# Two broadcast rows of an mLSTM stage, loaded by chunk of 128 tokens in place of by tile of 256

## The chip, the cores and the metric

The kernel runs on one core of a Trainium2 chip. The metric is the device time of one execution in microseconds (us), as the median of several runs. The profile is of one execution. Its engines are called PE (matrix multiplications, with PEld for its weight loads), DVE (VectorE), ACT (ScalarE), POOL (GpSimd) and SP (SyncE, which here issues nearly all DMAs).

## What is computed

The reference applies two blocks to x [1, 2048, 1024], in float32. The first is a gated linear attention block with its own normalization. The second is a hybrid layer: one projection feeds three mixers, an mLSTM, a sliding-window attention and a stick-breaking attention, and their outputs are joined, projected, normed and added to x. The change lies in the mLSTM. For each head it does, chunk by chunk (the kernel takes 128 tokens, the reference 64; the result is the same in exact arithmetic):

```python
b = cumsum(log_f);  dmat = b[t] - b[s] + log_i[s]  (s <= t);  inter = b + m
m_t = max(inter, max_s dmat)
s = (q @ k.T) * exp(dmat - m_t)
num = exp(inter - m_t) * (C @ q) + s @ v;  den = exp(inter - m_t) * (n @ q) + sum(s)
h = num / max(|den|, exp(-m_t))
C, n, m = the state carried to the next chunk, scaled by the factor of its last token
```

Two quantities depend on the query token t: `b - m_t`, and the factor `exp(inter - m_t)`. On the chip the token t lies along the free dimension of the tiles that need them, so each has to be present on all partitions, as a broadcast row: bc0 and bc1.

## The kernel before, in words

The work goes in stages over tiles of T = 256 tokens, NT = 8 tiles a stage: GLA twice, an output projection, then sliding-window attention, mLSTM, stick-breaking attention and the last projection. Nearly all matrix products are taken three times with parts of the numbers (`dense3`, lines 276 to 278), and PE is the engine that is busiest.

In a stage `pipeline` (line 177) runs three generators side by side: `mix(t)`, the recurrent part of tile t, beside `gate(t)` and `dense(t + 1)`, the projections of the same and of the next tile. The generators only set the order in which the program names its instructions. Then a planner, which simulates the time of each instruction, puts them in order on each engine: an instruction that it takes to be ready can go ahead of one that stands earlier in the program and isn't. On the chip each engine, and SP with its DMAs, works through its fixed order and waits where an operand is not there yet.

For the mLSTM, `dense(t)` is `mlstm_dense` (line 1197). It makes u and v, the convolution, and then calls `mlstm_stats` (line 1124), which works on a [4, 2, 128] tile (heads by two chunks). It writes `b - m_t` to the DRAM tensor `rows[0]` (line 1149, 4 KB), adds the carried m and takes the exponential in the same tile, and writes that to `rows[1]` (line 1155, 4 KB). DVE's addition at line 1153 has to wait until the first write has read the tile. Back in `mlstm_dense`, lines 1254 to 1257 load both rows from DRAM with a broadcast over 128 partitions:

```python
bc.append(wk.tile([128, 4, T], F32, name=f"bc{j}", tag=f"bc{j}", bufs=2 - j))
nc.sync.dma_start(bc[j], self.rows[j:j + 1, :, t * T:t * T + T].to_broadcast([128, 4, T]))
```

Each load is 512 KB, in 128 x 4 pieces of 1 KB (256 tokens of one head); `rows` is [2, 4, 2048], so the rows of the heads lie 8 KB apart. bc0 has two buffers, bc1 one. The store of the mLSTM output (line 1302, `yT<-ym`) is on SP too; the loads of the next tiles' hidden states (line 234, hh and hl) are issued by POOL.

`mix(t)` calls `mlstm_chunk` (line 1309) for chunks i = 0 and 1. ACT makes w as four exponentials of bc0 (line 1319, recorded at the helper's line 134), POOL masks it (line 1320), PE makes the scores st (1324), DVE multiplies (1325). POOL makes qw = qT * bc1 (line 1330), and PE adds w @ v (1332) and qw @ C (1334) in the bank nu. POOL scales the old state by the last column of the chunk in bc1 (line 1349), DVE adds the new part (1351). Chunk 0 of tile 0 has no state yet, so it does not read bc1.

qT and kT are copied out of PSUM by ACT for two heads (line 1269) and by DVE for two (line 1271); the PSUM tag qk has one bank, so PE's next products at line 1267 wait for that copy.

Of the kernel before, what the change touches and what calls it, by code (L numbers as in the profile page):

```python
# [8 lines left out]
F32 = mybir.dt.float32  # L9
# [17 lines left out]
def interleave(a, na, b, nb):  # L27
    """run the generators a (na steps) and b (nb steps) side by side"""
    ia = ib = 0
    while a is not None or b is not None:  # L30
        if b is None or (a is not None and ia * nb <= ib * na):
            if next(a, StopIteration) is StopIteration:
                a = None
            ia += 1
        else:
            if next(b, StopIteration) is StopIteration:
                b = None
            ib += 1


class Bank:
    """accumulation groups side by side in one PSUM bank: its first matmul clears the bank"""
# [13 lines left out]
class ConstPool:  # L56
    """single tiles by name"""
# [8 lines left out]
class K:  # L66
# [45 lines left out]
    def open(self, ctx, name, bufs=2, side=None):  # L112
        """SBUF of a phase"""
        return ctx.enter_context(self.tc.tile_pool(name=name, bufs=bufs, side=side, reuse_waits="tile"))

    def psum(self, ctx, name, **banks):
        """the PSUM banks of a phase by tag; mm: beside the two lasting ones"""
        self.banks = banks
        self.pp = ctx.enter_context(self.tc.tile_pool(name="ps_" + name, bufs=1, space=PSUM, reuse_waits="tile"))

    def behind(self, ins, before):
        """issue order on one engine, no wait"""
        self.tc.add_manual_dep(ins, before.name, mybir.DependencyInfo(mybir.DependencyClass.NoSync,
                                                                      mybir.DependencyReason.DATA), reason="table")

    def table(self, name):
        """the activation tables that the following Exp, Ln or Sigmoid use"""
        self.tab = self.nc.scalar.preload_act_table_set(name).ins
        for i in self.acts:
            self.behind(self.tab, i)  # L130
        self.acts = []
# [18 lines left out]
    def weights(self, src, name, stage=None, pool=None, k0=0, k1=None, more=None):  # L150
        """src: DRAM [128, k, n]; returns the hi and lo parts of rows k0 to k1. stage: gives the staging tiles;
        more: DRAM [128, k, m] of further columns"""
# [24 lines left out]
    def pipeline(self, n, load, dense, nd, gate, ng, mix, nm, first, lead=0, nxt=None, pri=0):  # L177
        """beside mix(t) run gate(t, h of t) and dense(t + 1, h of t + 1); load(t) gives h two tiles ahead.
        nd, ng, nm(t): the steps of dense, gate and mix; lead: gate goes first for so many t;
        first: h of tile 0 and its dense, begun or None. nxt: what follows: its load(0), its weights, its dense  # L180
        and the steps of it that go here; returns h, weights and the dense begun"""
# [36 lines left out]
    def ahead(self, steps, n):  # L218
        """the steps, their instructions picked as if they stood n earlier"""
        done = False  # L220
        while not done:
            with self.tc.high_priority(offset=n) if n else nullcontext():
                done = next(steps, StopIteration) is StopIteration
            if not done:
                yield

    def load_hl(self, src):
        """src: DRAM hi and lo [128, NK, T] each"""
        out = []
        for n, d in zip(("hh", "hl"), src):  # L230
            out.append([])
            for j in range(0, NK, 4):
                x = self.hp.tile([128, 4, T], F32R, name=n, tag=n)
                self.nc.gpsimd.dma_start(x, d[:, j:j + 4, :])
                out[-1] += [x[:, i, :] for i in range(4)]
        return out

    def load_h(self, src, pool, n, bufs, tag="hf"):
        """src: DRAM [128, NK, T] -> hi, lo; by n rows"""
        for k in range(0, NK, n):  # L240
            h = pool.tile([128, n, T], F32, name="hf", tag=tag, bufs=bufs)
            self.nc.sync.dma_start(h, src[:, k:k + n, :])
            yield k, h

    def split_h(self, parts, B=None):
        """parts: (k, float32 [128, n, T]) -> hi, lo of them, plus the columns B if given"""
# [17 lines left out]
    def dense3(self, out, a, ca, b, cb):  # L264
        """out = sum over k of a[:, k, ca].T @ b[:, k, cb], float32 from three passes."""
        for _ in self.dense3_steps(out, a, ca, b, cb):
            pass

    def dense3_steps(self, out, a, ca, b, cb):
        """the same, with a stop in the middle"""  # L270
# [9 lines left out]
    def rstd(self, out, ss, n):  # L280
        """out = (ss / n + EPS) ** -0.5"""
# [4 lines left out]
    def silu_col(self, src, n, name):  # L286
        """silu of a [128, n] tile by exp and ln."""
# [8 lines left out]
    def matvec(self, pool, w, c, col0):  # L296
        """acc[p, j] = sum over k of c[k * 128 + p] * w[k * 128 + p, col0 + j], j < 512"""
# [11 lines left out]
    def mod_cols(self, pool, stage, w, c, name, at):  # L309
        """columns: G = g * (1 + scale), B = shift, each [128, NK] (feature k * 128 + p). at: (k, what to do there)"""  # L310
# [43 lines left out]
    def transposed(self, xs, tag):  # L354
        """xs: two [128, D] token tiles -> (k, two rows of 128 features in a PSUM bank)"""
# [8 lines left out]
    def make_h(self, pool, banks, G, B, tags=(("hn", 2),) * 4):  # L364
        """banks: of transposed tokens (already scaled by rstd) -> float32 times the columns G, plus B if given,
        by two rows of 128 features"""
# [15 lines left out]
    def x_rstd(self, wk, i, keep):  # L382
        """token-major x, or its squares, and the rstd of its rows"""
# [20 lines left out]
    def x_normed(self, wk, t, G):  # L404
        """feature-major x times rstd and the columns G, by two rows of 128 features"""
# [12 lines left out]
    def gla_consts(self, wk):  # L418
# [7 lines left out]
        # the gate's low-rank part, token-major: hi, hi, lo, each with a column for the bias  # L426
# [76 lines left out]
    def late_mod(self, wk, j):  # L503
        """512 columns of: gate of block 1, shift, scale and gate of block 2"""
# [28 lines left out]
    def gla_dense(self, wk, t, hs, W, st):  # L533
# [6 lines left out]
        # token-major v and r; the low-rank gate  # L540
# [6 lines left out]
        if t % NT == 0:  # L547
            # its rows from partition 0 and 64: hi, from 32: lo, to meet the gate's hi, lo and hi
# [78 lines left out]
        # v of the second head  # L627
# [8 lines left out]
    def gla_gate(self, wk, t, hs, W, st):  # L636
        """silu of r"""
# [11 lines left out]
    def gla_mix(self, wk, t, st, ST):  # L649
# [4 lines left out]
        # scores of both heads and both 128-token chunks  # L654
# [75 lines left out]
    def units(self, key):  # L730
        """loads of the four weight units of a phase"""
# [3 lines left out]
    def halves(self, W):  # L735
        """units of half the rows -> all rows"""
        return [[a + b for a, b in zip(W[j], W[j + 1])] for j in range(0, len(W), 2)]
# [65 lines left out]
    def fm(self, out, W, c0, hs):  # L803
        """feature-major block: out [128 columns from c0, T]"""
        self.dense3(out, W, slice(c0, c0 + 128), hs, slice(0, T))

    def stack_k(self, ka, kb, pk, cols):
        """pk [128, T]: two heads on the partition halves; their hi and lo parts, each head stacked on 128"""
# [6 lines left out]
    def stack_q(self, qs, pq):  # L815
        """pq [128, T]: two heads on the partition halves. qs [128, 4, T]: by head, hi on both halves;
        then by head, lo on the half of its k's hi, zero on the other"""
# [8 lines left out]
    def qk(self, out, qs, h, qt, ks):  # L826
        """out = q.T @ k of head h; ks: columns of its stacked k"""
# [81 lines left out]
    def stick_rows(self, wk, n, b, q, i, kst, v, zero, y, st, po, bank):  # L909
        """queries n * 128 .. of heads 2b and 2b + 1 against all keys before them, from the last chunk back"""  # L910
# [55 lines left out]
    def silu_exp(self, out, src, tmp):  # L966
        """out = src * sigmoid(src), tmp of the same shape"""
# [156 lines left out]
    def mlstm_stats(self, wk, t, g, mp):  # L1124
        """g: gate pre-activations [128, chunk, 8] of tile t -> per-token exponents by chunk and head:
        for the columns, for the state, exp(-m)"""
# [70 lines left out]
    def mlstm_dense(self, t, hs, W):  # L1197
# [8 lines left out]
        def values():  # L1206
            """v, token-major with a column of ones, and the gates"""
# [47 lines left out]
        for j in range(2):  # L1255
            bc.append(wk.tile([128, 4, T], F32, name=f"bc{j}", tag=f"bc{j}", bufs=2 - j))
            nc.sync.dma_start(bc[j], self.rows[j:j + 1, :, t * T:t * T + T].to_broadcast([128, 4, T]))
        # q and k of each head
# [50 lines left out]
    def mlstm_chunk(self, wk, c, i, st, Cs, hg):  # L1309
        qT, kT, vs, bc, y, mst = st[:6]  # L1310
# [7 lines left out]
        for h in range(4):  # L1318
            self.act(w[:, h, :], bc[0][:, h, tok], AF.Exp, bias=mst[:, i, 0, h:h + 1])
# [8 lines left out]
        if Co is not None:  # L1328
            qw = wk.tile([96, 4, 128], F32, name="qw", tag="qw", bufs=1)
            nc.gpsimd.tensor_tensor(qw, qT[:, :, tok], bc[1][0:96, :, tok], op=OP.mult)  # L1330
# [5 lines left out]
        if not last:  # L1336
# [11 lines left out]
            else:  # L1348
                nc.gpsimd.tensor_tensor(Cn, Co, bc[1][0:96, :, i * 128 + 127:i * 128 + 128].to_broadcast([96, 4, 97]),
# [4 lines left out]
        # h = num / max(|den|, exp(-m)), normed over the head  # L1354
# [61 lines left out]
    def rstd_newton(self, sm, n):  # L1416
        """sm [128, 4]: column 3 = (column 2 / n + EPS) ** -0.5, from the exponent's estimate on"""
# [18 lines left out]
# (index of the padded weight, 128-row block) per mLSTM head of 96 rows  # L1436
# [3 lines left out]
def prep(inp):  # L1440
    """layout only"""
# [83 lines left out]
```

## Time and profile before

| | |
|---|---|
| median of 3 runs | 2237.99 us (2236.0 to 2239.27) |
| span of the profiled execution, first to last instruction | 2235.3 us |
| PE busy | 2131.8 us, 95% |
| mLSTM stage | about 1240 to 1640 us of the span |

The span is of one execution, profiled apart from the three timed runs; its own time outside of the span is not recorded, and the median of the runs is 2.7 us above the span. A "mean ns" or "busy" of an engine counts the instruction alone. "Idle before, releaser" says how long the engine stood still before an instruction and what ended that. A wait is put down to the last thing waited for.

### The profile page before, as it was taken

How to read it: one execution, taken by the hardware profiler on the slowest of the kernel's cores; microseconds unless marked ns; L12 is line 12 of the kernel's file. 1: busy time of each engine (PE TensorE's matmuls, PEld its weight loads, DVE VectorE, ACT ScalarE, POOL GpSimd, SP SyncE). 2: the span in 40 equal slices, each digit the busy share in tenths (PEclk: the TensorE clock that was granted, in tenths of full speed). 3: DMA queues.
4: the chain of work that ended last, by engine and by line, in shares of the span. 5: the costliest groups of instructions: out<-in, count | busy, mean ns of one | idle time of the engine just before them, and what ended most of it. 6: DMA issues, size and time to landing. Idle time of an engine off the chain costs nothing. (4 is left out here: it accounts for less than half of the span.)

```text
span 2235.3 us, 39197 instructions
## 1 busy us (share of the span) xinstructions
PE 2131.8 (95%) x14912; PEld 1902.3 (85%) x14912; DVE 1356.7 (61%) x2517; ACT 902.1 (40%) x2290; POOL 857.7 (38%) x1362
## 2 busy tenths in 40 slices
PE   6999999999999999899999999889799999999998
PEld 6899998899998788797888898888798888777787
DVE  6755756566656466564545455445456688788843
ACT  3534334333333333354545343433445555554411
POOL 3522335322223455553324322232445454573410
PEclk9999999999999999999999999989899999999999
DMA  9522313423322566751214322332441111122252
GB/s 321 178 67 73 126 55 114 123 82 99 91 67 91 195 210 225 241 165 53 90 46 145 98 65 72 84 99 67 121 130 43 44 44 43 44 67 81 67 175 99
DMA packets 122412, 240.00 MB, mean 107 GB/s; under 512 B 13248, under 2 KB 39782, under 8 KB 122224
## 3 DMA queue, kind: packets, MB, share of 16 engines
q1 hardware_dynamic: 108400, 187.17, 27.1%
q0 software_dynamic: 13824, 50.34, 7.1%
q8 instruction: 117, 1.92, 0.4%
q14 instruction: 71, 0.58, 0.1%
HBM read 178.66 MB, written 58.79 MB: 106 GB/s over the span
## 5 line engine op out<-in xcount | busy, mean ns | idle before, releaser
L937 DVE TENSOR_TENSOR_SCAN ke<-ke,zero 128x512 f32<-128x512 f32 (+3 forms) x160 | 186.9, 1182 | 25.9 <-POOL ke L932 14.1
L276 PE MATMUL mm<-hh,u1h 128*128 128x256 f32 x640 | 189.1, 296 | 0.0
L278 PE MATMUL mm<-hh,u1l 128*128 128x256 f32 x640 | 187.9, 294 | 0.0
L277 PE MATMUL mm<-hl,u1h 128*128 128x256 f32 x640 | 186.6, 292 | 0.0
L276 PE MATMUL mm<-u0h,hh 128*128 128x272 f32 (+2 forms) x464 | 155.1, 334 | 5.7 <-POOL hh L260 3.6
L278 PE MATMUL mm<-u0h,hl 128*128 128x272 f32 (+2 forms) x464 | 153.9, 332 | 0.6 <-DVE hl L261 0.4
L277 PE MATMUL mm<-u0l,hh 128*128 128x272 f32 (+2 forms) x464 | 153.6, 331 | 0.0
L276 PE MATMUL mm<-hh,u2h 128*128 128x256 f32 x512 | 147.3, 288 | 0.8 <-DVE gs L564 0.5
L277 PE MATMUL mm<-hl,u2h 128*128 128x256 f32 x512 | 146.4, 286 | 0.0
L278 PE MATMUL mm<-hh,u2l 128*128 128x256 f32 x512 | 145.7, 286 | 0.0
L278 PEld LDWEIGHTS mm<-hh,u1l 128*128 128x128 f32 x640 | 126.0, 197 | 1.3 <-issue 0.9
L276 PEld LDWEIGHTS mm<-hh,u1h 128*128 128x128 f32 x640 | 126.0, 197 | 0.7 <-issue 0.2
L277 PEld LDWEIGHTS mm<-hl,u1h 128*128 128x128 f32 x640 | 125.6, 196 | 0.7 <-issue 0.3
L276 PE MATMUL mm<-u3h,hh 128*128 128x256 f32 (+1 forms) x384 | 124.3, 324 | 0.8 <-DVE vl L546 0.8
L278 PE MATMUL mm<-u3h,hl 128*128 128x256 f32 (+1 forms) x384 | 123.3, 321 | 0.0
L277 PE MATMUL mm<-u3l,hh 128*128 128x256 f32 (+1 forms) x384 | 122.7, 319 | 0.0
L49 PE MATMUL po<-aT,sv 128*64 128x128 f32 x1088 | 108.9, 285 | 6.6 <-DVE aT L952 4.9
L134 ACT ACTIVATE be<-z 128x512 f32<-128x512 f32 (+3 forms) x160 | 86.0, 538 | 68.3 <-PE aT L947 68.0
L276 PE MATMUL mm<-hh,u3h 128*128 128x256 f32 x384 | 110.4, 287 | 0.5 <-POOL u3h L147 0.5
L277 PE MATMUL mm<-hl,u3h 128*128 128x256 f32 x384 | 110.3, 287 | 0.0
L278 PE MATMUL mm<-hh,u3l 128*128 128x256 f32 x384 | 109.3, 285 | 0.2 <-DVE mprev L1189 0.2
L134 ACT ACTIVATE ke<-z 128x512 f32<-128x512 f32 (+3 forms) x160 | 86.1, 541 | 54.8 <-PE z L830 33.1
(419 smaller groups left out, 6983.9 us busy)
## 6 DMA issues: line engine op xcount, KB each, us to landing
hh<-h2Th POOLq DMA_DIRECT2D x48, 512.0 KB, 6.0
hl<-h2Tl POOLq DMA_DIRECT2D x48, 512.0 KB, 5.3
mvw<-in_mod_w SPq DMA_DIRECT2D x48, 256.0 KB
stage<-in_ada_w SPq DMA_DIRECT2D x32, 256.0 KB
xt<-in_x SPq DMA_DIRECT2D x16, 512.0 KB
stage<-in_gla_w SPq DMA_DIRECT2D x32, 256.0 KB
oT<-oT SPq DMA_DIRECT2D x32, 256.0 KB
hf<-hT SPq DMA_DIRECT2D x32, 256.0 KB
```

The lines of the kernel that those rows point to most:

```text
L49: i = self.k.nc.tensor.matmul(out, a, b, start=first is None, stop=stop, skip_group_check=True).ins
L134: i = self.nc.scalar.activation(out, src, func, **kw).ins
L276: mm(out, ah[k][:, ca], bh[k][:, cb], start=(k == 0), stop=False)
L277: mm(out, ah[k][:, ca], bl[k][:, cb], start=False, stop=False)
L278: mm(out, al[k][:, ca], bh[k][:, cb], start=False, stop=(k == NK - 1))
L937: nc.vector.tensor_tensor_scan(ke[:, 0:w][:, ::-1], ke[:, 0:w][:, ::-1], zero.to_broadcast([128, w]), ke[:, w:w + 1], op0=OP.mult, op1=OP.add)
```

## The change

The two rows are loaded by chunk: per tile two loads of bc0 with 128 partitions, [128, 4, 128], and two of bc1 with 96 partitions, in pieces of 512 B. In the program they stand in the order bc0 of chunk 0, bc1 of chunk 0, bc0 of chunk 1, bc1 of chunk 1. Each of the two tags has three buffers of half the size, so the SBUF taken is the same (12 KB a partition). `mlstm_chunk` takes the tiles of its chunk. Nothing else is changed but comments.

```diff
         bc = []
-        for j in range(2):
-            bc.append(wk.tile([128, 4, T], F32, name=f"bc{j}", tag=f"bc{j}", bufs=2 - j))
-            nc.sync.dma_start(bc[j], self.rows[j:j + 1, :, t * T:t * T + T].to_broadcast([128, 4, T]))
+        for i in range(2):
+            ts = slice(t * T + i * 128, t * T + i * 128 + 128)
+            bc.append([])
+            for j, n in ((0, 128), (1, 96)):
+                x = wk.tile([128, 4, 128], F32, name=f"bc{j}", tag=f"bc{j}", bufs=3)
+                nc.sync.dma_start(x[0:n], self.rows[j:j + 1, :, ts].to_broadcast([n, 4, 128]))
+                bc[i].append(x)
...
-        qT, kT, vs, bc, y, mst = st[:6]
+        qT, kT, vs, bcs, y, mst = st[:6]
+        bc = bcs[i]
...
-            self.act(w[:, h, :], bc[0][:, h, tok], AF.Exp, bias=mst[:, i, 0, h:h + 1])
+            self.act(w[:, h, :], bc[0][:, h, :], AF.Exp, bias=mst[:, i, 0, h:h + 1])
...
-            nc.gpsimd.tensor_tensor(qw, qT[:, :, tok], bc[1][0:96, :, tok], op=OP.mult)
+            nc.gpsimd.tensor_tensor(qw, qT[:, :, tok], bc[1][0:96], op=OP.mult)
...
-                nc.gpsimd.tensor_tensor(Cn, Co, bc[1][0:96, :, i * 128 + 127:i * 128 + 128].to_broadcast([96, 4, 97]),
+                nc.gpsimd.tensor_tensor(Cn, Co, bc[1][0:96, :, 127:128].to_broadcast([96, 4, 97]),
```

## Rows read from the trace of the kernel before

**Rows 1.** The page: the span, busy time of PE's two queues and of the other engines (share of the span, instructions).

```profile
span 2235.3 us, 39197 instructions
...
PE 2131.8 (95%) x14912; PEld 1902.3 (85%) x14912; DVE 1356.7 (61%) x2517; ACT 902.1 (40%) x2290; POOL 857.7 (38%) x1362
```

**Rows 2.** The view by windows, the mLSTM stage: the stretch and its length, busy time (and number of instructions) of PE, PEld, DVE, ACT and POOL, the mean granted clock of PE as a share of full speed, the busy share of the DMA engines, GB/s.

```profile
1240.00:1640.00 400.00, 354.46 (x2650) 344.01 (x2649) 194.23 (x423) 155.99 (x461) 125.45 (x179) 0.93 0.35 91
```

**Rows 3.** The view of waits, PE alone, 1240 to 1640 us: who waited for whom, us in total, times, longest.

```profile
PE nu L1334 <- POOL qw L1330: 28.2, 6, 6.7
PE nu L1332 <- DVE w L1325: 8.9, 3, 3.7
PE qk L1267 <- ACT qT L1269: 6.1, 2, 3.2
```

**Rows 4.** The view of waits of the other engines in the same stretch, and of SP's queue from 1257 to 1600 us, with the same columns.

```profile
ACT w L134 <- DMA bc<-rows: 52.3, 8, 9.2
...
POOL Cn L1349 <- DMA bc<-rows: 24.3, 5, 5.8
...
POOL qw L1330 <- DMA bc<-rows: 16.8, 3, 5.8
...
SPq L1257 <- DMA rows<-lfR: 65.5, 16, 7.8
```

**Rows 5.** The time line of SP's queue: start, us to issue, line, what is loaded or stored. First tile 2, then tile 4, 5 and 6. Of the two loads at L1257 the first is bc0, the second bc1; of the two stores, L1149 is rows[0], L1155 rows[1].

```profile
1350.60 0.36 SPq L1257 DMA_DIRECT2D bc<-rows  x1
1351.02 0.50 SPq L1302 DMA_DIRECT2D yT<-ym  x1
1351.57 0.42 SPq L1155 DMA_DIRECT2D rows<-lfR  x1
...
1435.45 0.26 SPq L1149 DMA_DIRECT2D rows<-lfR  x1
1436.69 0.36 SPq L1257 DMA_DIRECT2D bc<-rows  x1
1437.66 0.26 SPq L1155 DMA_DIRECT2D rows<-lfR  x1
1444.13 0.36 SPq L1257 DMA_DIRECT2D bc<-rows  x1
...
1485.49 0.36 SPq L1257 DMA_DIRECT2D bc<-rows  x1
...
1492.94 0.36 SPq L1257 DMA_DIRECT2D bc<-rows  x1
...
1533.26 0.36 SPq L1257 DMA_DIRECT2D bc<-rows  x1
...
1540.85 0.36 SPq L1257 DMA_DIRECT2D bc<-rows  x1
```

**Rows 6.** The time lines of ACT, POOL and PE at the first use of the rows: start, us, line, operation, out<-in, shapes, number of instructions merged, idle time before and what ended it. Tile 4, then POOL's first use of bc1 in tiles 5 and 6.

```profile
1444.95 2.45 ACT L134 ACTIVATE w<-bc,mst 128x128 f32<-128x128 f32 x8 [5.07 <-DMA bc<-rows]
...
1453.81 0.83 POOL L1349 TENSOR_TENSOR Cn<-Cn,bc 96x388 f32<-96x388 f32 x1 [5.78 <-DMA bc<-rows]
...
1455.21 1.25 POOL L1330 TENSOR_TENSOR qw<-qT,bc 96x512 f32<-96x512 f32 x1
...
1456.51 0.74 PE L1334 MATMUL nu<-Cn,qw 96*128 96x97 f32 x2 [6.47 <-POOL qw L1330]
...
1459.97 1.27 POOL L1330 TENSOR_TENSOR qw<-qT,bc 96x512 f32<-96x512 f32 x1 [0.41 <-PE nu L1334]
...
1501.78 0.83 POOL L1349 TENSOR_TENSOR Cn<-Cn,bc 96x388 f32<-96x388 f32 x1 [5.41 <-DMA bc<-rows]
...
1549.07 0.83 POOL L1349 TENSOR_TENSOR Cn<-Cn,bc 96x388 f32<-96x388 f32 x1 [4.74 <-DMA bc<-rows]
```

**Rows 7.** The time lines of ACT and PE in tiles 0 and 1, with the same columns.

```profile
1272.61 0.57 ACT L1269 ACTIVATE qT<-qk 96x512 f32<-96x512 f32 x1
...
1273.23 0.36 PE L1267 MATMUL qk<-cuh,wqh 128*96 128x256 f32 x1 [2.92 <-ACT qT L1269]
...
1314.88 0.57 ACT L1269 ACTIVATE qT<-qk 96x512 f32<-96x512 f32 x1
```

**Rows 8.** The view by windows, with the columns of rows 2: the stream of bc0 in tile 4 with no other load beside it; tile 4's wait and the work after it; the load of bif (after its first us); a store of oT to DRAM in pieces of 512 B.

```profile
1438.00:1443.00 5.00, 5.00 (x45) 4.82 (x44) 1.22 (x5) 0.59 (x1) 1.02 (x1) 1.00 0.42 83
1444.00:1460.00 16.00, 9.53 (x71) 9.37 (x70) 2.59 (x5) 4.37 (x12) 5.58 (x10) 0.76 0.63 166
972.00:973.00 1.00, 1.00 (x9) 1.00 (x10) 0.72 (x3) 0.95 (x2) 1.00 (x3) 1.00 0.05 3
134.90:136.10 1.20, 1.20 (x12) 1.20 (x11) 0.54 (x3) 0.38 (x1) 0.00 (x0) 1.00 0.71 219
```

**Rows 9.** Other broadcasts. From the list of DMA issues (KB each): the gate row of block 1 over 128 partitions in pieces of 4 KB, and bif, 8 numbers over 128 partitions in pieces of 32 B. From the time lines of SP and DVE: the issue of the gate and its first use.

```profile
gate<-gate SPq DMA_DIRECT2D x1, 512.0 KB
...
bif<-in_m_bif SPq DMA_DIRECT2D x1, 4.0 KB
...
750.33 0.50 SPq L740 DMA_DIRECT2D gate<-gate  x1
...
756.17 1.90 DVE L768 TENSOR_TENSOR xr<-mm,gate 128x512 f32<-128x512 f32 x3 [11.73 <-DMA gate<-gate]
```

## The prediction

> **What bounds the kernel now.** The first view is the page: TensorE (PE) is busy for 2131.8 of 2235.3 us and no other engine passes 61% [rows 1]. So time is won or lost only where PE waits, or works at a lower clock. The second view is the row of the mLSTM stage among the windows: in the 400 us from 1240 to 1640 PE is busy for 354.46, so 45.5 us are lost there, and the mean granted clock is 0.93 [rows 2]. The third is the table of PE's waits in that stretch: 28.2 us in six waits of the matmuls at L1334 for qw, 8.9 in three for w, 6.1 in two for the ScalarE (ACT) copy of qT [rows 3]. The reader is to see that all three end in the broadcast rows. POOL's multiplications at L1330 and L1349 wait for DMA bc, and ACT's exponentials wait 52.3 us for it [rows 4]; the ACT copy of qT at 1272.61 and 1314.88 only stands in line behind these exponentials, and PE waits for the copy [rows 7].
>
> The fourth view is the time line of tile 4, for why the rows come late [rows 5, 6]. SP issues bc0 at 1436.69, the write of rows[1] at 1437.66, and bc1 only at 1444.13, since bc1 reads what that write stores: 65.5 us of SP's waits at L1257 are for the DMA of rows [rows 4]. ACT starts at 1444.95, POOL at 1453.81, PE goes on at 1456.51 after 6.47 us. The write of 4 KB took 6.47 us, where the same write of rows[0], with nothing ahead of it, took 1.24 (1435.45 to 1436.69). It waited behind bc0: 512 KB at 83 GB/s, as the window 1438 to 1443 has it [rows 8], are 6.3 us of stream, and 0.97 + 6.47 = 7.44 is that stream plus about 1.2. I call the stream of bc0 6.2 us, which leaves exactly 1.24 beside it. From bc0's issue to POOL's first use of bc1 it is 17.12 us in tile 4, 16.29 in tile 5, 15.81 in tile 6, mean 16.4; from bc1's own issue 9.68, 8.84 and 8.22, mean 8.9, which is a stream of 6.2 and 2.7 beside it [rows 5, 6]. ACT's start is 8.26 after bc0's issue, 6.2 + 2.06.
>
> The single buffer of bc1 is not what holds it. Were it so, SP would wait at L1257 for POOL, whose last use of the old bc1 comes before; its waits there are for the DMA [rows 4].
>
> **The change, part by part.** (1) *The third buffer and the split of tiles* remove waits for a free buffer that do not exist: nothing. (2) *Two issues become four.* Each costs SP 0.37 us [rows 5]. Two of them, 0.74 us, fit in the 0.97 between bc0's issue and that of rows[1], where SP has nothing else: nothing, and 0.4 a tile if the write slips. (3) *bc1 for 96 partitions* removes a quarter of its bytes. (4) *Pieces of 512 B in place of 1 KB.* This is the disputed price. Bytes per tile fall from 1024 to 2 x (256 + 192) = 896 KB, pieces rise from 1024 to 2 x (512 + 384) = 1792. Let S be the stream of one chunk of bc0; bc1's is then 0.75 S.
>
> The trace has no 512 B broadcast, so S has bounds. If bytes rule, S is half of 6.2: 3.1. If pieces rule, S is 6.2. The nearest rows: 83 GB/s in pieces of 1 KB are 81 pieces a us, 12.3 ns each; the broadcast bif, 128 pieces of 32 B, ran at 3 GB/s [rows 8, 9], some 94 a us, 10.7 ns each (78 to 109 with the rounding). A piece of 1/32 of the size costs almost as much; between these two, 512 B gives 11.4 ns and S = 5.85. On the other side the broadcast of the gate, 512 KB in 128 pieces of 4 KB, was used 5.84 us after its issue; less 1.24 that is 36 ns a piece, against (8.26 - 1.24) / 512 = 13.7 for 1 KB; the line through these two gives 10.0 ns at 512 B, S = 5.1 [rows 5, 6, 9]. That issue of the pieces is not the limit is shown by the store of oT, at 219 GB/s [rows 8]. I take S = 5.4, near both lines, and keep 3.1 and 6.2 as ends.
>
> (5) *The order on SP.* In the code the write of rows[1] stands ahead of all loads, yet SP has bc0 ahead of it: a load goes when the planner has it ready. Both chunks of bc0 need only rows[0], so I expect bc0 of chunk 0, bc0 of chunk 1, rows[1], then bc1 of chunks 0 and 1. In tile 2 another DMA, the store of ym, did get into that gap [rows 5]. The write of rows[1] then stands behind two streams, and bc1 of chunk 0 is issued at 2S + 1.24 after bc0, used at 2S + 1.24 + 0.75S + 2.7 = 2.75S + 3.94. With S = 5.4 that is 18.8 against 16.4: 2.4 us later. Break-even is S = 4.5. What queues behind SP's longer wait is the store of ym (nobody near waits for it) and, in tile 7, the loads of c_w.
>
> (6) *ACT.* The exponentials of chunk 1 now wait for the second load: start 2S + 2.06, end 1.2 later (half of the 2.45 for eight), 14.1 at S = 5.4 against 8.26 + 2.45 = 10.7 now. The 3.4 us are hidden where PE waits for qw anyway (tiles 2 to 7), and show in tiles 0 and 1, where the copy of qT stands behind them. bc1 of chunk 1 comes 0.75S = 4.1 us after that of chunk 0. Its cover is the work of chunk 0: in tile 4 POOL needs the second qw 4.8 us after the first [rows 6]. It costs nothing, and up to some 3 us a tile if that cover shrinks.
>
> **Sum.** Six tiles (2 to 7) by 2.4 are 14.4, two tiles by 3.4 are 6.8: +21.2 us. The clock already falls in each such wait (0.76 over 1444 to 1460 [rows 8]), so a longer wait adds no second fall. The profiled span of 2235.3 becomes 2256.5; the median of the runs is 2.7 above the span, and I carry that over: 2259. With S = 5.1 the same sum is 6 x 1.6 + 2 x 2.8 = 15, 2253; with S = 4.6 it is 6 x 0.2 + 2 x 1.8 = 5, 2243; with S = 6.2, 6 x 4.6 + 2 x 5 = 38, 2276. This case's own range is 2243 to 2276.
>
> **The rivals.** *Bytes rule* (S = 3.1): use at 12.5, 3.9 earlier in six tiles, 23.4, and 1.2 in two: -26, 2212. For it: half the bytes lie ahead of the first use. The waits could hold it: in tiles 4 to 7 they are 5.0 to 6.7 us. Against it: the 10.7 ns of bif. It decides below S = 4.5. Chance 0.17. The Trainium skill, DMA: Bandwidth & Descriptors, "Why small descriptors are slow (HBM only)", charges a packet its bytes over 32 plus about 3 cycles. By that, an estimate from the page, 512 B cost 19 cycles against 35, S would be 3.4 and the time some 2217. Its "Specifications" name 512 B as the least piece for the full rate. The trace does not bear that rule out: 1 KB and 32 B pieces of a broadcast differ by 1.6 ns, not by a factor of 9.
>
> *The order is another*: rows[1] and bc1 of chunk 0 ahead of bc0 of chunk 1. Use at 1.75S + 3.94 = 13.4, 3.0 earlier, six tiles -18, 2220; ACT's chunk 1 then comes later still, and up to 8.7 us in two tiles give it back, 2237. It would need the planner to hold a ready load. Chance 0.13.
>
> *No difference*: rows[1] slips in between the two loads of bc0, so that only the ring is longer for bc1: 2.75S + 2.7. With S = 5.1 that is 16.7, 0.3 later, 2 us in six tiles; ACT's 2.8 in two tiles come on top if the copy of qT stays behind the exponentials. 2240 to 2246, two thirds of it within 4.5 us. It decides between S = 4.6 and 5.2. For it: rows[1] is ready only 0.6 us after SP is free. Chance 0.17.
>
> *The forecast*, chance 0.53.
>
> **How the numbers follow.** About 0.2% (4.5 us) is what a measurement of this kernel can tell from no change. Slower: the forecast but for its lowest edge, 0.49, and a third of the third rival, 0.06, are 0.55. Faster: the bytes, 0.17, and most of the other order, 0.11, are 0.28. The rest, 0.17, is the same. The range has to reach into the faster cases: 2213 to 2276 leaves out about half of the bytes rival and the little above 2276.
>
> **What would show it.** In the profile after: four loads of bc a tile, the second bc0 ahead of rows[1]; rows[1] to the first bc1 longer than 6.5 us (11 by the forecast); POOL's first use of bc1 some 18.8 us after the first bc0; PE's waits at L1334 above 28.2 us, some 42; the GB/s of a lone chunk stream near 48 (pieces at 5.4 us) and not 83. The forecast is wrong if that stream runs at 83 GB/s, if rows[1] is issued ahead of the second bc0, or if PE's waits at L1334 shrink while these hold, because its order was planned anew.

## The result, and the profile after

| | before | after |
|---|---|---|
| median of the runs, timed side by side | 2237.09 us | 2262.45 us |
| ratio, with its 95% interval | | 1.0105 [1.0089, 1.0121] |
| span of the profiled execution | 2235.3 us | 2262.1 us |

One of the four runs of the kernel after took 3392.92 us at a granted clock of 0.559; the ratio leaves it out, and the median of the other three is 2261.05 us. The change makes the kernel some 24 us slower (25.4 by the medians of the table). First the page of the kernel after: the span, and the engines' busy time.

```profile
span 2262.1 us, 39220 instructions
...
PE 2137.3 (94%) x14912; PEld 1907.7 (84%) x14912; DVE 1354.9 (60%) x2517; ACT 903.4 (40%) x2290; POOL 856.9 (38%) x1362
```

PE has the same 14912 matmuls as in [rows 1], 5.5 us more busy time, and 26.8 us more span. Next the mLSTM stage alone, from the first store of rows[0] to the first scan of the next stage, in the view by windows. Before:

```profile
1259.74:1635.92 376.18, 330.64 (x2483) 323.26 (x2482) 176.82 (x387) 145.63 (x436) 115.13 (x154) 0.92 0.33 86
```

After:

```profile
1264.08:1661.72 397.64, 334.01 (x2483) 326.50 (x2482) 177.05 (x387) 146.63 (x435) 114.62 (x154) 0.89 0.28 79
```

The stage is 21.5 us longer: 18.1 more us in which PE stands still, and 3.4 us more for the same 2483 matmuls, at a clock of 0.89 in place of 0.92. Of the other 5.3 us of span, 4.3 lie ahead of the stage, where both programs are the same. Its start falls between 1257.6 and 1264.4 us in the profiles of this study, early and late both with loads by chunk and by tile, so these 4.3 us are not put down to the change.

Who PE waits for in the stage after, and ACT's and POOL's waits for the loads, in the view of waits (us in total, times, longest):

```profile
PE nu L1339 <- POOL qw L1335: 28.2, 6, 11.2
PE nu L1337 <- DVE w L1330: 20.1, 5, 5.1
PE qk L1271 <- ACT qT L1273: 12.1, 3, 6.0
...
ACT w L134 <- DMA bc<-rows: 68.5, 16, 7.1
POOL Cn L1354 <- DMA bc<-rows: 59.7, 6, 11.4
POOL qw L1335 <- DMA bc<-rows: 10.7, 2, 6.0
```

Against [rows 3] the wait for qw has the same sum, but its longest has gone from 6.7 to 11.2; the waits for w have grown by 11.2 us and those for the copy of qT by 6.0. These three are 17.2 us more, nearly all of the 18.1. Behind them POOL and ACT wait longer for the loads than in [rows 4].

Now SP's time line after, tile 2 and then tile 4:

```profile
1358.45 1.01 SPq L1260 DMA_DIRECT2D bc<-rows  x2
1360.13 0.27 SPq L1155 DMA_DIRECT2D rows<-lfR  x1
1360.45 0.94 SPq L1306 DMA_DIRECT2D yT<-ym  x1
1375.00 0.85 SPq L1260 DMA_DIRECT2D bc<-rows  x2
...
1458.07 0.93 SPq L1260 DMA_DIRECT2D bc<-rows  x2
1459.09 0.35 SPq L1155 DMA_DIRECT2D rows<-lfR  x1
1466.99 0.86 SPq L1260 DMA_DIRECT2D bc<-rows  x2
```

The order is the forecast one: both chunks of bc0, rows[1], both chunks of bc1. In tile 4 the write of rows[1] takes 7.90 us (6.47 in [rows 5]); bc1 is issued 8.92 us after bc0, not 7.44. In tile 2 the same step takes 14.87 us. The stream itself in tile 4, in the view by windows: five us of the first chunk, then two in which the second runs beside it.

```profile
1459.00:1464.00 5.00, 5.00 (x44) 4.82 (x43) 1.61 (x5) 0.60 (x2) 1.12 (x2) 1.00 0.22 40
1464.00:1466.00 2.00, 2.00 (x19) 2.00 (x18) 0.69 (x1) 0.14 (x1) 0.00 (x0) 1.00 0.40 109
```

The stream in pieces of 512 B runs at 40 GB/s, that is 78 pieces a us; with pieces of 1 KB it was 83 GB/s, 81 a us [rows 8]. Half the bytes take the same time. (Both chunks are issued ahead of this window. That 40 GB/s is the rate of a chunk alone is shown below, where the second is held back.) The DMA engines are 22% busy meanwhile (0.22, the last column but one), as a mean of all 16; how the pieces spread over them is not in the trace.

POOL's and PE's time lines in tile 4 of after:

```profile
1473.57 0.83 POOL L1354 TENSOR_TENSOR Cn<-Cn,bc 96x388 f32<-96x388 f32 x1 [10.68 <-DMA bc<-rows]
1474.36 0.63 POOL L1325 TENSOR_SCALAR_AFFINE_SELECT w<-w 128x512 f32<-128x512 f32 x1
...
1476.09 0.66 POOL L1325 TENSOR_SCALAR_AFFINE_SELECT w<-w 128x512 f32<-128x512 f32 x1
1476.69 1.28 POOL L1335 TENSOR_TENSOR qw<-qT,bc 96x512 f32<-96x512 f32 x1
...
1475.78 0.46 PE L1337 MATMUL nu<-v,w 128*128 128x97 f32 x2 [4.38 <-DVE w L1330]
1478.02 0.74 PE L1339 MATMUL nu<-Cn,qw 96*128 96x97 f32 x2 [1.78 <-POOL qw L1335]
```

POOL uses bc1 15.50 us after bc0's issue, 1.6 us sooner than the 17.12 of [rows 5, 6]. But the planner has now put the scaling of the state, which waits for bc1, ahead of both masks of w, which do not need it. So the mask waits for a load that it does not read, PE waits for w first, and its matmul with qw starts 19.95 us after bc0's issue, as before (19.82).

Tile 4 does not stand for the others. By tile, from the same views (us; the first line is the time from the issue of the first bc0 to POOL's first use of bc1):

| tile | 2 | 3 | 4 | 5 | 6 | 7 |
|---|---|---|---|---|---|---|
| first use of bc1, before | 16.98 | 15.64 | 17.12 | 16.29 | 15.81 | 19.53 |
| first use of bc1, after | 23.51 | 15.74 | 15.50 | 15.60 | 16.20 | 20.18 |
| PE's waits for w and qw, before | 4.7 | 5.0 | 6.5 | 5.5 | 5.0 | 10.4 |
| PE's waits for w and qw, after | 10.7 | 6.3 | 6.2 | 6.0 | 6.6 | 12.5 |

More than half of the 11.2 us that PE waits longer for w and qw lies in tile 2. There the write of rows[1] is 14.87 us old when bc1 is issued (8.32 before), and the loads of hh and hl, issued at 1359.87 and 1360.46, and the store of ym run beside it; before, the last load of hh was issued at 1346.82, ahead of bc0. That these hold the write up is not tested. In tiles 3 to 6 bc1 moves by 0.1, -1.6, -0.7 and 0.4 us and the waits by 1.3, -0.3, 0.5 and 1.6. So by these rows POOL's new order costs about 1.2 us a tile there, some 5 in all. Two more places, tile 0 (ACT, then PE) and tiles 2 and 7 (PE):

```profile
1278.14 1.28 ACT L134 ACTIVATE w<-bc,mst 128x128 f32<-128x128 f32 x4 [2.51 <-DMA bc<-rows]
1279.32 0.57 ACT L1273 ACTIVATE qT<-qk 96x512 f32<-96x512 f32 x1
...
1279.95 0.53 PE L1271 MATMUL qk<-cuh,wqh 128*96 128x256 f32 x1 [5.29 <-ACT qT L1273]
...
1383.28 0.74 PE L1339 MATMUL nu<-Cn,qw 96*128 96x97 f32 x2 [10.71 <-POOL qw L1335]
...
1632.83 0.74 PE L1339 MATMUL nu<-Cn,qw 96*128 96x97 f32 x2 [11.23 <-POOL qw L1335]
```

### The profile page after: what moved, and what is told of

The parts are those of the page before. It is cut to its first block, busy times and chain, and to the rows that moved or that the text cites. A ratio compares the mean times of both kernels' runs of the same rounds, so it can differ in the third digit from the quotient of the medians.

```text
span 2262.1 us, 39220 instructions
## 1 busy us (share of the span) xinstructions
PE 2137.3 (94%) x14912; PEld 1907.7 (84%) x14912; DVE 1354.9 (60%) x2517; ACT 903.4 (40%) x2290; POOL 856.9 (38%) x1362
## 5 line engine op out<-in xcount | busy, mean ns | idle before, releaser
L937 DVE TENSOR_TENSOR_SCAN ke<-ke,zero 128x512 f32<-128x512 f32 (+3 forms) x160 | 186.3, 1177 | 26.9 <-POOL ke L932 14.4
```

What stands on the lines that cost most here:

```text
L937: nc.vector.tensor_tensor_scan(ke[:, 0:w][:, ::-1], ke[:, 0:w][:, ::-1], zero.to_broadcast([128, w]), ke[:, w:w + 1], op0=OP.mult, op1=OP.add)
```

## The experiments

Theory A, the prediction's: the streams' length, by their number of pieces, decides when bc1 is there. Theory B: what counts is the order planned anew on POOL (and, in tiles 0 and 1, ACT's line). The ratios are to runs of the kernel before beside each kernel, with medians from 2236.43 to 2238.71 us.

**Only bc0 by chunk.** bc1 is one load and one buffer, as before. The edit is to the kernel after.

```diff
...
-            for j, n in ((0, 128), (1, 96)):
-                x = wk.tile([128, 4, 128], F32, name=f"bc{j}", tag=f"bc{j}", bufs=3)
-                nc.sync.dma_start(x[0:n], self.rows[j:j + 1, :, ts].to_broadcast([n, 4, 128]))
-                bc[i].append(x)
+            x = wk.tile([128, 4, 128], F32, name="bc0", tag="bc0", bufs=3)
+            nc.sync.dma_start(x, self.rows[0:1, :, ts].to_broadcast([128, 4, 128]))
...
+        x = wk.tile([128, 4, T], F32, name="bc1", tag="bc1", bufs=1)
+        nc.sync.dma_start(x, self.rows[1:2, :, t * T:t * T + T].to_broadcast([128, 4, T]))
...
```

> Only bc0 is loaded by chunk (two loads of 256 KB, three buffers); bc1 stays one load of 512 KB in one buffer. Theory A (the write of rows[1] stands behind both loads of bc0 and pieces rule): in tile 4 of the changed kernel bc1 was issued 8.92 us after bc0 against 7.44 before, so the same here, 1.5 us in six tiles and some 3 us in tiles 0 and 1 through ScalarE's line: about +15 us on the kernel before, 2252. Theory B (the planner's new order on GpSimd and PE is what costs, the transfers hardly): it depends on the order that it draws here; if the mask of w stays ahead of the state's scaling as before, under +8, 2237 to 2245.

Measured: 2268.02 us, 1.0136 [1.0116, 1.0157]. The waits of PE:

```profile
PE nu L1341 <- POOL qw L1337: 56.2, 6, 11.9
PE qk L1273 <- ACT qT L1275: 11.4, 3, 5.6
```

The split of bc0 alone costs more than the whole change: it doubles the wait for qw and nearly doubles that for the copy of qT ([rows 3]: 28.2 and 6.1). That is A's direction, and 16 us more than it expected. In tiles 2 to 7 POOL's first mask stands ahead of the scaling, as before, so B's case of under +8 falls. POOL's first use of bc1 comes 1.0 us later than before in tile 4 and 2.8 to 4.2 later in tiles 3, 5 and 6.

**Only bc1 by chunk.** bc0 is one load into two buffers, bc1 is two loads over 96 partitions into two. The edit is to the kernel after; the loads that it replaces are not shown.

```diff
+        x = wk.tile([128, 4, T], F32, name="bc0", tag="bc0", bufs=2)
+        nc.sync.dma_start(x, self.rows[0:1, :, t * T:t * T + T].to_broadcast([128, 4, T]))
...
+            x1 = wk.tile([128, 4, 128], F32, name="bc1", tag="bc1", bufs=2)
+            nc.sync.dma_start(x1[0:96], self.rows[1:2, :, ts].to_broadcast([96, 4, 128]))
```

> Only bc1 is loaded by chunk and for 96 partitions (two buffers of half a tile, so that it fits); bc0 stays one load of 512 KB. Theory A: the write of rows[1] waits for one stream of 6.2 us as before, bc1 of chunk 0 is issued at 7.4 and, at 0.75 of the pieces, used about 2.5 us earlier in six tiles: some -12, 2225. Theory B: the scaling of the state now stands ahead of the mask of w on GpSimd and eats that: within 5 us of the kernel before. Either way tiles 0 and 1 (ScalarE's line) should be as before, some 6 us of PE's waits for the copy of qT.

Measured: 2232.05 us, 0.998 [0.9968, 0.9992].

```profile
PE nu L1340 <- POOL qw L1336: 16.8, 6, 5.2
PE nu L1338 <- DVE w L1331: 14.6, 6, 3.2
PE qk L1272 <- ACT qT L1274: 7.2, 2, 4.4
```

The first bc1 comes sooner and the wait for qw falls by 11.4 us from [rows 3], but 5.7 of these come back as waits for w, since POOL's order is again the new one. So A's gain is there, and B takes half of it. The two halves of the change, +29.9 and -6.0 us against before, make 23.9, close to the whole.

**POOL's order by hand.** The kernel after, with mask of w, qw, then scaling of the state.

```diff
+        sel = nc.gpsimd.affine_select(w, w, ...).ins
...
+            iq = nc.gpsimd.tensor_tensor(qw, ...).ins
+            self.behind(iq, sel)
...
+                ic = nc.gpsimd.tensor_tensor(Cn, Co, ...).ins
+                self.behind(ic, iq)
```

> The changed kernel with GpSimd's order fixed by hand in each chunk: mask of w, then qw, then the scaling of the state (which waits for the same load as qw but is needed later). Transfers and all else unchanged. Theory B: in tiles 3 to 6 the mask no longer stands behind the load of bc1 and qw starts at its landing; PE goes on some 3 us earlier in each, -12 us, 2250, and PE's waits for w at the numerator fall from 20.1 to under 8. Theory A: the loads come when they come; qw alone moves by 0.8 + 0.6, at most -5, 2257.

Measured: 2244.11 us, 1.0029 [1.0018, 1.004], so 0.76% of the time of before, some 17 us, come back. The waits of PE:

```profile
PE nu L1340 <- POOL qw L1335: 36.2, 6, 10.2
PE qk L1271 <- ACT qT L1273: 12.5, 3, 6.2
...
PE nu L1338 <- DVE w L1330: 1.2, 1, 1.2
```

The wait for w goes from 20.1 to 1.2 us, and 8.0 of that come back at qw. B holds for that part: the order on POOL, with the same loads, makes PE wait for w. But the written order is not that of before either, which in tiles 3 to 6 had the scaling ahead of qw (tile 4 in [rows 6]). So the 17 us are not all a cost of the change.

**The second bc0 behind the first bc1.** The order of the prediction's second rival, on the kernel after.

```diff
+                d = nc.sync.dma_start(x[0:n], ...).ins
+                if (i, j) == (0, 1):
+                    first = d
+                elif (i, j) == (1, 0):
+                    self.behind(d, first)
```

> The changed kernel with SP's order of the loads as in the program: the second load of bc0 behind the first of bc1, and so behind the write of rows[1]. This is the rival of the prediction (2220 to 2237). Theory A with pieces ruling: a lone chunk of 512 pieces at 84 a us takes 6.1, so rows[1] lands no sooner than before, bc1 of chunk 0 is used some 14 us after the first bc0 (15.5 in the changed kernel), and the exponentials of chunk 1 start some 17 us after it (11.5): a gain of 1 to 2 in tiles 2 to 7, a loss of 5 in tiles 0 and 1, 2258 to 2266. Theory of bytes: 2220.

Measured: 2277.8 us, 1.0179 [1.0162, 1.0196]. ACT's exponentials of chunk 1 now come last, and PE waits for what stands behind them. The lines are PE's waits, and the first chunk of bc0 in tile 4, which here has no other load beside it:

```profile
PE nu L1343 <- POOL qw L1339: 30.5, 5, 7.7
PE nu L1341 <- DVE w L1334: 16.8, 6, 3.8
PE qk L1275 <- ACT qT L1277: 14.4, 2, 13.7
PE st L1333 <- DVE qT L1279: 5.6, 1, 5.6
...
1467.00:1471.00 4.00, 4.00 (x36) 3.82 (x35) 1.05 (x4) 0.59 (x1) 1.02 (x1) 1.00 0.24 40
```

The rival's 2220 to 2237 us falls: what it gains at bc1 it loses at the second bc0. In tile 4 POOL uses bc1 13.43 us after the first bc0 (15.50 in the kernel after), but the second exponentials start at 20.49 us (11.53 after). A expected 17 for these, and its 2258 to 2266 us is missed too. The lone chunk runs at 40 GB/s, and bc1 is issued 7.36 us after it, as before with a whole tile (7.44): so half the bytes do take the same time.

**The copy of qT first on ACT.** The kernel after, with the exponentials of w ordered behind the copy of qT of the same tile (`st[7]`; the expectation calls it the next tile's).

```diff
...
+            iw = self.act(w[:, h, :], bc[0][:, h, :], AF.Exp, ...)
+            self.behind(iw, st[7])
```

> The kernel after, with ACT's exponentials of w ordered behind its copy of the next tile's qT. If the exponentials that stand ahead of that copy and wait for the second chunk's broadcast are what tiles 0 and 1 lose, the waits for qT fall from 12.1 to under 4 us and the time by 5 to 10 us, to 2252 to 2258 us. If the copy was late for another reason, or PE then waits for w instead, the time stays within 3 us of 2262 us.

Measured: 2248.88 us, 1.0052 [1.0037, 1.0067]; PE's wait for that copy is 0.8 us.

```profile
PE nu L1341 <- POOL qw L1337: 27.9, 6, 11.3
PE nu L1339 <- DVE w L1332: 23.4, 7, 4.9
...
PE qk L1272 <- ACT qT L1274: 0.8, 1, 0.8
```

0.53%, some 12 us, come back, more than was expected, and the waits for qw and w stay (28.2 and 20.1 in the kernel after). ACT's line is a cause of its own. About half of its wait, 6.1 of 12.1 us, was there before the change [rows 3].

**Both orders.** The two edits together.

> The kernel after, with POOL's order (mask of w, qw, scaling of the state) and ACT's order (exponentials of w behind the copy of qT) both written out. If the two losses lie in different tiles they add up (each alone gave back 18.3 and 13.6 us of 2262.4): 2228 to 2234 us, a little below before. If they are partly the same wait: 2238 to 2246 us.

Measured: 2234.57 us, 0.9977 [0.9961, 0.9993]. The two gains, 0.76% and 0.53%, make 1.29%, and 1.28% arrive: they add up. With both lines written out the kernel takes the time of before. That does not show that the split by itself is free on these streams, since before with the same two orders was not run, and the run with only bc0 by chunk speaks against it. Waits for qw of 39.6 us remain. Why are they there at all? The next runs take up the streams.

**Rows stored by tile.** The kernel before; a broadcast of a tile is 128 pieces of 4 KB.

```diff
-        self.rows = dram("rows", [2, 4, S])
+        self.rows = dram("rows", [2, NT, 4 * T])
...
-            nc.sync.dma_start(bc[j], self.rows[j:j + 1, :, t * T:t * T + T].to_broadcast([128, 4, T]))
+            nc.sync.dma_start(bc[j].rearrange("p h k -> p (h k)"), self.rows[j, t:t + 1, :].to_broadcast([128, 4 * T]))
```

> The kernel before, with the two rows stored by tile, so that a broadcast of a whole tile is 128 pieces of 4 KB (before: 512 of 1 KB; after: 512 and 384 of 512 B a chunk). Theory A, the stream's time goes by its number of pieces: the first broadcast's stream shrinks from about 6 us towards 2 to 3 us, the second row's store and the second broadcast come earlier by as much, and PE's waits for qw (28.2 us before) fall below 12 us: 2208 to 2225 us. Rival, the stream goes by its bytes (some 83 GB/s): the stream still takes about 6 us, the waits stay, and the time is 2234 to 2242 us.

Measured: 2180.75 us, 0.9744 [0.9721, 0.9767], far below what either theory expected. The stream of bc0 in tile 4:

```profile
1411.50:1413.50 2.00, 2.00 (x19) 1.82 (x18) 0.85 (x3) 0.45 (x1) 0.01 (x1) 1.00 0.67 252
```

It is 252 GB/s in place of 83, so the bytes were not what held it at 83. The stage is 316.58 us long, with 309.78 busy at a clock of 0.99.

**No rows loaded.** The kernel before with w and qw made from zeros; this part of the computation is left out.

```diff
-            nc.sync.dma_start(bc[j], ...)
...
+                nc.gpsimd.memset(x, 0.0)
```

The memset is done once for each of the two tiles, ahead of the stage.

> The kernel before without any load of the two rows: w and qw are made from tiles of zeros, so this part of the computation is left out; the rows are still made and stored. It bounds what all waiting for the broadcasts costs. If PE's waits in the stage are nothing else than these loads, the 43 us of waits for qw, w and qT nearly go: 2195 to 2205 us. If other work is late next (the chain over the state, ACT's exponentials), some 15 to 25 us of them stay: 2210 to 2225 us.

Measured: 2176.59 us, 0.9727 [0.9701, 0.9753]. With no load there is 61 us less, 18 more than PE's 43.2 us of waits in [rows 3]. Rows by tile get all but 4 of them.

**The same on the kernel after.** Rows stored by chunk: pieces of 2 KB.

```diff
-        self.rows = dram("rows", [2, 4, S])
+        self.rows = dram("rows", [2, NT, 2, 4 * 128])
...
-                nc.sync.dma_start(x[0:n], self.rows[j:j + 1, :, ts].to_broadcast([n, 4, 128]))
+                nc.sync.dma_start(x[0:n].rearrange("p h k -> p (h k)"), self.rows[j, t, i:i + 1, :].to_broadcast([n, 512]))
```

> The kernel after, with the rows stored by chunk, so that a chunk's broadcast is 128 (or 96) pieces of 2 KB instead of 512 (or 384) of 512 B; the four loads a tile, the buffers and what may go ahead of what stay as in the change. Theory A, the change loses by its small pieces: without them it gains what the run with 4 KB pieces by tile gained, 2178 to 2190 us. Rival, the loads by chunk cost something by themselves (four loads, SP's order, POOL's plan): 2195 to 2225 us.

Measured: 2178.61 us, 0.9727 [0.971, 0.9743]. The loads by chunk cost nothing by themselves, and gain nothing that can be told from the run by tile.

**Small pieces without the change.** The kernel before, whole tiles, but 1024 pieces of 512 B for each, 1 KB apart in DRAM.

```diff
-        self.rows = dram("rows", [2, 4, S])
+        self.rows = dram("rows", [2, NT, 8, 256])
...
+            nc.sync.dma_start(bc[j].rearrange("p h (c k) -> p (h c) k", c=2),
+                              self.rows[j, t:t + 1, :, 0:128].to_broadcast([128, 8, 128]))
```

> The kernel before, whole tiles and its own buffers and order, but with the rows stored with gaps so that a tile's broadcast is 1024 pieces of 512 B (before: 512 of 1 KB). Theory A, the time of a stream goes by its pieces: a broadcast's stream takes some 12 us instead of 6, the second row and its broadcast come 6 us later in each of the eight tiles, and as waiting lowers the granted clock too, the stage loses 50 to 85 us: 2285 to 2325 us. Rival, the stream goes by its bytes: 2234 to 2245 us.

Measured: 2180.56 us, 0.973 [0.971, 0.9751], where theory A expected over 2285. One us of the stream of bc0:

```profile
1418.50:1419.50 1.00, 1.00 (x11) 0.98 (x11) 0.41 (x2) 0.45 (x1) 0.00 (x0) 1.00 1.08 327
```

327 GB/s in pieces of 512 B are 640 pieces a us, eight times the 78 to 81 of before and after. A's rule on the number of pieces falls, and the bytes rule with it: what differs is where the pieces lie.

**One number.** The kernel after with S + 256 columns, so that the heads lie 9 KB apart and not 8. Theory C of the expectation is that the 8 KB make the streams slow, its rival D that any distance of several KB does.

```diff
-        self.rows = dram("rows", [2, 4, S])
+        self.rows = dram("rows", [2, 4, S + 256])
```

> The kernel after with one number changed: the rows in DRAM have S + 256 columns, so the four heads of a chunk lie 9 KB apart and not 8 KB; pieces (512 B), loads, buffers and orders are those of the change. The run with whole tiles in 512 B pieces within 8 KB has already shown that small pieces alone cost nothing. Theory C, the streams are slow because the four heads lie 8 KB apart: the first broadcast's stream falls to about 2 us, the waits go as with the other layouts, 2174 to 2188 us. Rival D, any heads that lie several KB apart are slow, since the pieces must lie close together: the time stays at 2255 to 2264 us.

Measured: 2181.63 us, 0.9758 [0.9732, 0.9783]. Theory C holds, D falls. The time lines of SP and POOL in tile 4:

```profile
1411.78 0.93 SPq L1260 DMA_DIRECT2D bc<-rows  x2
1412.80 0.35 SPq L1155 DMA_DIRECT2D rows<-lfR  x1
1415.53 1.33 SPq L1260 DMA_DIRECT2D bc<-rows  x2
...
1418.49 0.84 POOL L1354 TENSOR_TENSOR Cn<-Cn,bc 96x388 f32<-96x388 f32 x1 [1.89 <-DMA bc<-rows]
1419.29 0.63 POOL L1325 TENSOR_SCALAR_AFFINE_SELECT w<-w 128x512 f32<-128x512 f32 x1
```

The windows of the two bc0 loads in tile 4, both in flight, and of the stage:

```profile
1413.00:1415.00 2.00, 2.00 (x19) 1.82 (x18) 0.84 (x4) 0.47 (x1) 0.00 (x0) 1.00 0.80 236
...
1257.64:1580.20 322.56, 312.61 (x2483) 307.34 (x2482) 175.76 (x387) 145.94 (x436) 114.74 (x154) 0.98 0.31 97
```

PE's wait for qw in the stage:

```profile
PE nu L1339 <- POOL qw L1335: 7.4, 2, 5.3
```

The write of rows[1] is back in 2.73 us, not 7.90, with the same two loads of 512 pieces ahead of it. POOL's order is still scaling before mask, but its wait is 1.89 us and no longer 10.68. The stage is 75.1 us shorter than in after.

**Rows by tile and both orders.** The run with pieces of 4 KB, with POOL's and ACT's order written out.

> The run with 4 KB pieces by whole tile, with POOL's order written out (mask of w, qw, then scaling of the state) and ACT's exponentials ordered behind the copy of qT. If the three costs (stream, POOL's order, ACT's line) are separate, the gains add up: 5 to 12 us below the run with 4 KB pieces alone. If the wide pieces have already taken away what POOL and ACT wait for, the two are within 3 us of each other; if the written order makes something else late, this one is slower.

Measured: 2183.06 us, 0.9754 [0.9735, 0.9772], 2.3 us from the run without the orders: once the loads come quickly, neither order matters.

The versions with another spacing, 2178.61 to 2183.06 us, beat both kernels, and they lie within 6.5 us of no load at all.

## Why the prediction was right, and where it was not

The time, 2259 for 2262.45, and the direction are right; the sum is right only in part. It had 21.2 us, and the stage grew by 21.5, but from other terms.

- *What bounds the stage* (broadcast rows behind all three waits): right. Without the loads, or with quick ones, the waits are nearly gone. The price of a wait was set too low: the prediction gave a longer wait no cost in clock, and the 18.1 us more of waiting came with 3.4 us more of busy time. With the waits gone the price is larger. From before to the run with one number changed, PE stands still 35.6 us less in the stage (45.5 to 9.9), and its 2483 matmuls take 18.0 us less (330.64 to 312.61, the clock from 0.92 to 0.98): half a us for each us of waiting that is gone.
- *Buffers, issues* (steps 1 and 2, nothing): no row speaks against them. Loads by chunk into three buffers cost and gain nothing once the streams are quick.
- *S, the stream of one chunk* (step 4, 5.4 us): set too short. 512 pieces at 78 a us are 6.5; by the prediction's own reckoning the lone chunk took 7.36 - 1.24 = 6.1, at the end of 6.2 where pieces rule. For this layout the number of pieces sets a lone stream, as forecast. As a rule on pieces it is wrong: 512 B pieces of the same broadcast run at 640 a us with another spacing. The rows that it was drawn from hid the variable. The gate's row lies in one piece, and its 36 ns a piece of 4 KB was no price of a stream: rows stored by tile, 4 KB pieces too, run at 252 GB/s, 16 ns a piece. Bif is slow for a reason that no run here settles. The rule of the Trainium skill, DMA: Bandwidth & Descriptors, "Why small descriptors are slow (HBM only)", by which a packet costs its bytes over 32 plus about 3 cycles, was set aside on these rows. By it, an estimate from the page, 512 B pieces would reach 86% of the rate of 4 KB pieces, and the runs with another spacing show no loss at all (327 GB/s in 512 B, 252 in 4 KB).
- *The order on SP* (step 5): right, in every tile. *Two streams end to end*, 2S = 10.8, is the term that failed: in tile 4 bc1 is issued 8.92 us after bc0 (9.07 to 9.58 in tiles 3, 5 and 6), so the two took some 7.7, although one alone took 6.1. The second ran beside the tail of the first (109 GB/s after 40). So in tile 4 bc1 was used 1.6 us sooner, not 2.4 later. The sign that followed from it, waits for qw of some 42 us, failed with it: they stayed at 28.2.
- *Where the 14.4 us of six tiles came from instead.* The waits for qw and w together grew by 11.2 us: 6.0 in tile 2, where rows[1] to bc1 takes 14.87, 3.1 in tiles 3 to 6 and 2.1 in tile 7. In tiles 3 to 6 the loads alone would have given some 2 us back, and POOL's new order took about 5; the prediction named a new plan only as what would make it wrong. So the sum agreed by luck: two streams set too long, one late tile and an order not foreseen replaced one another.
- *ACT's line in tiles 0 and 1* (step 6, 6.8 us): right. The wait for the copy of qT grew by 6.0, of it 5.2 in these two tiles, and some 12 us of time come back when the copy goes first and nearly the whole of this wait, old and new, is gone.
- *The rivals.* Bytes: excluded by the 40 GB/s. The other order: slower still, 2277.8 us. No difference: the second bc0 stands ahead of rows[1] in every tile, and the interval excludes it.

The cause under all this is the spacing of the rows: with the heads of a chunk 8 KB apart, a lone broadcast delivers about 80 pieces a us, of 1 KB and of 512 B alike. So a chunk takes as long as a tile did, and only the overlap of the two keeps bc0 from taking twice as long. The spacing was there before the change and cost the kernel before some 57 us. That it is the 8 KB, and not distance as such, is shown by the 9 KB. Which part of the path from DRAM is slow for these reads is not shown. The Trainium skill, DMA: Bandwidth & Descriptors, "Latency and other measured facts", reports slow copies for rows a large power of two apart, from 2 MiB on, and that padding by 4 KiB restores the rate; it supposes, unverified, that the streams alias on the memory's channels. It has the full rate at 512 KiB. Here a broadcast is slow at 8 KB and mended by 1 KB of padding; by the measurement such reads are slow at a much smaller distance, and whether the cause is the same is not shown.

## What to carry to other kernels

A small broadcast that took several us with the DMA engines 22 to 42% busy was limited by the spacing of its source, not by its bytes or the number of its pieces; before the size of such a load is changed, try a pad, which is one number. When loads are split, read each engine's planned order anew: an instruction that waits for a load in front of one that doesn't can eat the gain. And price a wait of PE with the clock that it loses, from the same matmuls' busy time in a stage with and without the waits.

## What the runs showed of the hardware that was not expected

- A broadcast of 512 B pieces runs at 40 GB/s alone when its four source rows lie 8 KB apart, and at 327 when its eight pieces lie 1 KB apart. Two of them, with the source rows 9 KB apart, run at 236 together.
- Two of the slow streams overlap: 40 GB/s for the first, 109, more than twice as much, once the second runs beside it.
- A 4 KB write behind them on SP's queue takes 7.90 us until the load that reads it is issued, and 2.73 behind the same loads with padded rows.
